# Layer norm's small chain in tensor-and-scalars operations, second half's loads moved up in the first stage, MLP gate's modulation on TensorE

## The chip, the cores and the metric

The kernel runs on one core of one Trainium2 chip. The metric is the device time of one execution in microseconds (us); lower is better. The engines of the core work at the same time, each through its own list of instructions in order, and wait for one another by semaphores: PE (TensorE, matrix products), DVE (VectorE), ACT (ScalarE), POOL (GpSimd) and SP (SyncE, which starts the transfers, DMAs).

## The reference

One step of a trunk of two layers over 128 context tokens and 512 latent tokens with 1024 features. A layer is a mixer and an MLP, each followed by a layer norm, and each modulated by (shift, scale, gate) rows that come from a conditioning vector through a large matrix. Cut to what matters here:

```python
mod_ctx = einsum('d,lde->le', silu(c_ctx), w_mod) + b_mod       # 6*1024 per layer, for the context
mod_lat = einsum('bd,lde->lbe', silu(c), w_mod) + b_mod         # and for the latents
def _layer_norm(x, g, b, eps=1e-5):
    mu, var = mean(x), mean(square(x - mu))
    return (x - mu) * rsqrt(var + eps) * g + b
def _block(x, mod, mixer, g, b, w1, w2):
    sh1, sc1, gt1, sh2, sc2, gt2 = split(mod, 6)                # kinds 0 to 5 below
    x = _layer_norm(ALPHA * x + gt1 * mixer(x * (1 + sc1) + sh1), g[0], b[0])
    ff = square(relu((x * (1 + sc2) + sh2) @ w1)) @ w2
    return _layer_norm(ALPHA * x + gt2 * ff, g[1], b[1])
```

The mixer of layer 0 (the even mixer) is retention beside differential attention, that of layer 1 (the odd mixer) is windowed attention with a sink beside gated linear attention (GLA), whose gates are summed up by scans in chunks of 16 tokens. All of it is in float32.

## The kernel before

The 640 tokens are five tiles of 128, t = 0 the context and t = 1 to 4 the latents. The program runs in stages: a start, the even mixer with its output projection, five layer norms, the MLP in eight groups, five norms, and the same for layer 1 with the odd mixer. The stages overlap at the seams, tile by tile.

Every large product is taken as three products of rounded parts, hi x hi, lo x hi and hi x lo. So each weight unit of 512 KB (`wraw`, three buffers) is split after it has landed: ACT casts the hi part (`whi`), DVE subtracts to get the lo part (`wlo`). Activations are split in the same way (`h0h` and `h0l`, `hh` and `hl`, and in the MLP `ghi` and `glo` from `relu`, the squared ReLU that DVE forms).

**Order of the work.** Nearly all instructions are recorded by helpers, so most rows carry one of few lines: 380 for DVE, ACT and POOL, 470 for matmuls, 485 for transposes, 454 for transfers. The order on PE, DVE, ACT and POOL comes from a planner (class `Order`) that follows a simulated clock while the program is written out. Chains of small steps are generators; a function `background` feeds in weight loads, splits and modulation steps when the clock is due: a modulation step every `MOD_SPACE` = 3.6 us, a chunk on PE every `MOD_PE` = 38 us of that clock. The start stage is different: its instructions stand on ACT, DVE and POOL in the order in which they are written (`order.fifo`). The transfers' queue on SP is ordered by a scheduler.

**Modulation rows.** A row of one kind has two chunks of 512 columns, and a chunk takes eight tiles of weights of 256 KB. Kinds 0 and 1 of layer 0 are made on PE in the start stage (`matvec`, weights `wmod` of the first half and then of the second half, results `mod`). Kinds 2, 3 and 4 of layer 0 are made on PE in the background of the even mixer (`ModPE`: two blocks of 16 small matmuls for a chunk, `modp`, from four buffers `wmodp`). All else (kind 5 of layer 0, the whole of layer 1, 14 chunks) is made by multiplying and adding on POOL, DVE and ACT (`ModChunk`: `wmod` times a column `cs` on POOL, added into `moda` on POOL; for the other accumulator one DVE operation `moda` in layer 1, or ACT `modp` and a POOL addition in layer 0), and summed over partitions by matmuls `modps`. Kind 5 of layer 0 is the gate of the first MLP, needed towards its end.

**Start stage.** The loads, splits and modulated tiles are written out by hand. The first half of the features is modulated (kind 1 and 0) and multiplied early (`early_part`) while the second half's modulation weights arrive.

**Layer norm.** `norm` takes statistics on DVE, the square root on ACT, and then refines 1 / sqrt(var + eps) by one Newton step on columns of [128, 1]: `r`, `q`, `r` again, and `nmr` = -mean * r. The large multiplies that follow (`x` times r plus nmr, then times and plus the rows `lnrow`) are shared by ACT, POOL and DVE. Only at the very end (`final`) are all five tiles written out at once; in the other norms, the next stage starts from the normalised tiles, and `x<-x,lnrow` is done later by POOL to rebuild the residual.

## Time and profile before

| | |
|---|---|
| time, median of 3 runs | 1669.2 us (1667.19 to 1670.53) |
| profiled execution's own time | 1671.51 us |
| its span, first to last instruction | 1669.7 us |
| mean granted clock of PE | 0.979 |
| busy, PE | 1579.6 us, 95% |
| busy, DVE | 1046.0 us, 63% |
| busy, ACT | 619.9 us, 37% |
| busy, POOL | 582.2 us, 35% |

The profiled execution has its own time, 1.8 us longer than its span. Matmuls are pipelined, so PE's busy share is a share of time and not of its peak. The granted clock is that of PE, as a share of full speed. The stages by their place in the span: start 0 to about 65 us, even mixer to about 330, its output projection and norms, first MLP from about 400 to 826, odd mixer from about 880 to 1130, second MLP to about 1651, and the last norms to the end.

### The profile page before, as it was taken

The page shows a single profiled execution, that of the slowest core. Times are in us where ns is not written, and L with a number is a line of the kernel's source. Part 1 is how long each engine was busy: PE and PEld are TensorE (multiplying, and loading weights), DVE is VectorE, ACT ScalarE, POOL GpSimd, SP SyncE. Part 2 cuts the span into 40 slices and gives each one's busy share as a digit, 9 for nine tenths or more (in the row PEclk, how much of TensorE's full clock was granted, in tenths as well). Part 3 has the DMA queues.
Part 4 walks back from the last instruction along what each step waited for, and adds up shares of the span by engine and source line. Part 5 has one row for each costly group of instructions (what it writes and reads, how often), then busy time and mean ns, then how long its engine had stood idle before and what let it go on. Part 6 is the DMA issues. An engine that isn't in the chain of part 4 may idle for free. (4 is left out here: it accounts for less than half of the span.)

```text
span 1669.7 us, 28365 instructions
## 1 busy us (share of the span) xinstructions
PE 1579.6 (95%) x11233; PEld 1431.6 (86%) x11233; DVE 1046.0 (63%) x1963; ACT 619.9 (37%) x1294; POOL 582.2 (35%) x493
## 2 busy tenths in 40 slices
PE   7999999999999999999898898979999999999995
PEld 4998999998989988998787887869989989998994
DVE  3777762685377667767877787777833334444458
ACT  2555443336433312221265454553543222222221
POOL 1110000111896687678557445340200110011215
PEclk9999999999999999999998998989999999999998
DMA  9523333332444444543424210014222221223121
GB/s 345 185 86 93 97 112 105 130 115 64 137 148 151 146 146 152 171 148 106 146 80 137 73 36 28 27 56 141 76 72 68 76 89 60 72 79 115 55 76 63
DMA packets 89764, 177.87 MB, mean 107 GB/s; under 512 B 23576, under 2 KB 30752, under 8 KB 89632
## 3 DMA queue, kind: packets, MB, share of 16 engines
q1 hardware_dynamic: 89632, 176.07, 32.6%
q8 instruction: 88, 1.44, 0.3%
q14 instruction: 44, 0.36, 0.1%
HBM read 169.53 MB, written 6.50 MB: 105 GB/s over the span
## 5 line engine op out<-in xcount | busy, mean ns | idle before, releaser
L470 PE MATMUL ff<-hh,whi 128*128 128x320 f32 (+2 forms) x960 | 297.1, 309 | 0.0
L470 PE MATMUL ff<-hh,wlo 128*128 128x320 f32 (+2 forms) x960 | 296.4, 309 | 0.1
L470 PE MATMUL ff<-hl,whi 128*128 128x320 f32 (+2 forms) x960 | 296.3, 309 | 0.0
L380 DVE TENSOR_TENSOR wlo<-wraw,whi 128x1024 fp32r<-128x1024 f32 (+1 forms) x183 | 243.3, 1334 | 80.4 <-ACT whi L380 80.2
L380 ACT CAST whi<-wraw 128x1024 fp32r<-128x1024 f32 (+1 forms) x183 | 189.5, 1045 | 278.8 <-PE fps L470 244.7
L470 PE MATMUL fps<-whi,glo 128*128 128x512 f32 (+1 forms) x648 | 254.3, 393 | 5.1 <-DVE glo L380 5.1
L470 PE MATMUL fps<-wlo,ghi 128*128 128x512 f32 (+1 forms) x648 | 253.7, 391 | 2.3 <-DVE wlo L380 2.3
L470 PE MATMUL fps<-whi,ghi 128*128 128x512 f32 (+1 forms) x648 | 254.9, 393 | 0.0
L380 POOL TENSOR_TENSOR x<-x,lnrow 128x512 f32<-128x512 f32 (+1 forms) x76 | 105.9, 1402 | 351.6 <-DVE y L380 214.5
L380 DVE TENSOR_TENSOR relu<-relu 128x320 f32<-128x320 f32 (+3 forms) x100 | 70.7, 707 | 186.6 <-ACT ghi L380 185.6
L470 PEld LDWEIGHTS ff<-hh,whi 128*128 128x128 f32 x960 | 180.2, 188 | 3.1 <-issue 2.1
L470 PEld LDWEIGHTS ff<-hl,whi 128*128 128x128 f32 x960 | 180.2, 188 | 0.6
L470 PEld LDWEIGHTS ff<-hh,wlo 128*128 128x128 f32 x960 | 180.2, 188 | 0.3 <-DVE wlo L380 0.3
L380 ACT ACTIVATE relu<-ff 128x320 f32<-128x320 f32 (+3 forms) x100 | 51.4, 514 | 278.7 <-PE ff L470 276.2
L380 DVE TENSOR_TENSOR y<-fps,y 128x512 f32<-128x512 f32 x120 | 82.7, 689 | 111.6 <-PE fps L470 111.5
L470 PEld LDWEIGHTS fps<-whi,glo 128*128 128x128 f32 x648 | 122.1, 188 | 33.2 <-DVE glo L380 5.5
L380 POOL TENSOR_TENSOR moda<-moda,wmod 128x512 f32<-128x512 f32 x98 | 146.0, 1490 | 6.8
L470 PEld LDWEIGHTS fps<-wlo,ghi 128*128 128x128 f32 x648 | 122.1, 188 | 30.3 <-DVE wlo L380 3.5
L470 PEld LDWEIGHTS fps<-whi,ghi 128*128 128x128 f32 x648 | 122.0, 188 | 29.0 <-issue 2.5
L380 POOL TENSOR_SCALAR wmod<-wmod,cs 128x512 f32<-128x512 f32 x98 | 112.7, 1150 | 92.8 <-DVE moda L380 81.4
L380 POOL TENSOR_TENSOR o<-o,sg 128x640 f32<-128x640 f32 x8 | 13.0, 1621 | 257.7 <-ACT o L380 257.3
L470 PE MATMUL proj<-whi,hh 128*128 128x256 f32 (+1 forms) x280 | 85.1, 304 | 12.5 <-DVE gm L380 7.6
(298 smaller groups left out, 3527.7 us busy)
## 6 DMA issues: line engine op xcount, KB each, us to landing
wraw<-in_w SPq DMA_DIRECT2D x128, 512.0 KB
wmod<-in_w_mod SPq DMA_DIRECT2D x144, 256.0 KB
wraw<-in_w_even SPq DMA_DIRECT2D x24, 512.0 KB
wmodp<-in_w_mod SPq DMA_DIRECT2D x48, 256.0 KB
wraw<-in_w_out SPq DMA_DIRECT2D x16, 512.0 KB
wraw<-in_w_odd SPq DMA_DIRECT2D x16, 512.0 KB
gate<-mrow SPq DMA_DIRECT2D x16, 256.0 KB
xT<-in_xT SPq DMA_DIRECT2D x8, 320.0 KB
```

Of the source, the lines that this page charges most:

```text
L380: i = f(*a, **k)
L470: nc.tensor.matmul(o, a, b, **kw)
```

## The change

Three edits. In `norm`, the steps on [128, 1] columns beside the square root are written with one tensor and scalars (constants or columns) each, and one of them is no longer needed: before `ve`, a reciprocal, `q`, `q` again, `r` and `nmr`, of which the last four read two tensors; now `veh`, a reciprocal in place, `q`, `r` and `nmr`. In the start stage, one unit's load and the row `dl` (for lambda, the factor of the differential attention) are asked for after the second half's modulation weights and `xT`, and the splits of the third and fourth unit and `lam` are done later. Kind 5 of layer 0 goes from `ModChunk` to `ModPE`, with `MOD_PE` 30 in place of 38. The diff:

```diff
@@ -37,9 +37,8 @@
 NSPL = 5
 DEC0, DEC = 0.0, 2.0
 MOD_SPACE = 3.6
-MOD_PE = 38.0
+MOD_PE = 30.0
 LO_POOL = 0
-DRS = False
 UPD = 30.0
 WD = 3
 WS = 2
@@ -412,7 +411,6 @@
     const = ctx.enter_context(tc.tile_pool(name="const", bufs=1))
     hpool = ctx.enter_context(tc.tile_pool(name="hpool", bufs=4))
     gpool = ctx.enter_context(tc.tile_pool(name="gpool", bufs=NSLOT))
-    mtmp = ctx.enter_context(tc.tile_pool(name="mtmp", bufs=1))
     mraw = ctx.enter_context(tc.tile_pool(name="mraw", bufs=MRAW))
     wraw = ctx.enter_context(tc.tile_pool(name="wraw", bufs=NRAW))
     wspl = ctx.enter_context(tc.tile_pool(name="wspl", bufs=NSPL))
@@ -596,13 +594,7 @@
                 act.activation(a0, raw, AF.Copy, scale=cs[:, k, 0:1])
                 pool.tensor_scalar(a1, raw, cs[:, k, 1:2], 0.0, op0=ALU.mult, op1=ALU.add)
             else:
-                if self.l == 0:
-                    tmp = mtmp.tile([P, 512], F32, tag="modp", name=nm("modp"))
-                    order.reuse("modp", 1, tmp)
-                    act.activation(tmp, raw, AF.Copy, scale=cs[:, k, 0:1])
-                    pool.tensor_tensor(a0, a0, tmp, op=ALU.add)
-                else:
-                    stt(a0, raw, cs[:, k, 0:1], a0, op0=ALU.mult, op1=ALU.add)
+                stt(a0, raw, cs[:, k, 0:1], a0, op0=ALU.mult, op1=ALU.add)
                 pool.tensor_scalar(raw, raw, cs[:, k, 1:2], 0.0, op0=ALU.mult, op1=ALU.add)
                 pool.tensor_tensor(a1, a1, raw, op=ALU.add)
             if k == KT - 1:
@@ -703,17 +695,15 @@
                 add_piece((l, "2", g, n), [Unit(io["w_2"][l, g, n, u], 2, 512) for u in range(2)])
     pos = [0, 0, 0]
     mod_steps = []
-    for l, kinds in ((0, (5,)), (1, range(6))):
-        if l < layers:
-            for c in kinds:
-                for a in range(2):
-                    chunk = ModChunk(l, 2 * c + a)
-                    mod_steps += [(chunk, k) for k in range(KT)]
+    for c in range(6 if layers > 1 else 0):
+        for a in range(2):
+            chunk = ModChunk(1, 2 * c + a)
+            mod_steps += [(chunk, k) for k in range(KT)]
     mod_left = [0.0, len(mod_steps)]
     mod_hold = [False]
     split_hold = [False]
 
-    mod_pe = [ModPE(2 * c + a) for c in (2, 3, 4) for a in range(2)]
+    mod_pe = [ModPE(2 * c + a) for c in (2, 3, 4, 5) for a in range(2)]
 
     def load_unit():
         units[pos[2]].load()
@@ -944,23 +934,14 @@
         for i, (a, c0, c1) in enumerate(cuts):
             dve.bn_stats(st[:, i, :], X[t][a][:, c0:c1])
         dve.bn_aggr(mv, st)
-        if DRS:
-            ve = sm("ve", [P, 1])
-            dve.tensor_scalar(ve, mv[:, 1:2], EPS, None, op0=ALU.add)
-            r = rsqrt(ve, [P, 1])
-        else:
-            ve = sm("ve", [P, 1])
-            sq = sm("sq", [P, 1])
-            act.activation(sq, mv[:, 1:2], AF.Sqrt, bias=eps_t)
-            dve.tensor_scalar(ve, mv[:, 1:2], EPS, None, op0=ALU.add)
-            r = sm("r", [P, 1])
-            q = sm("q", [P, 1])
-            dve.reciprocal(r, sq)
-            vec_tt(q, r, r, op=ALU.mult)
-            stt(q, q, -0.5, ve, op0=ALU.mult, op1=ALU.mult)
-            stt(r, q, 1.5, r, op0=ALU.add, op1=ALU.mult)
-        nmr = sm("nmr", [P, 1])
-        stt(nmr, mv[:, 0:1], -1.0, r, op0=ALU.mult, op1=ALU.mult)
+
+        veh, sq, q, r, nmr = (sm(n, [P, 1]) for n in ("veh", "sq", "q", "r", "nmr"))
+        act.activation(sq, mv[:, 1:2], AF.Sqrt, bias=eps_t)
+        dve.tensor_scalar(veh, mv[:, 1:2], EPS, -0.5, op0=ALU.add, op1=ALU.mult)
+        dve.reciprocal(sq, sq)
+        dve.tensor_scalar(q, sq, sq, veh, op0=ALU.mult, op1=ALU.mult)
+        dve.tensor_scalar(r, q, 1.5, sq, op0=ALU.add, op1=ALU.mult)
+        dve.tensor_scalar(nmr, mv[:, 0:1], -1.0, r, op0=ALU.mult, op1=ALU.mult)
         if not final:
             xn = X[t]
             for a in range(2):
@@ -1103,19 +1084,19 @@
     load_unit()
     xt = load_x(0)
     load_unit()
-    load_unit()
     ps = acc("mod0")
     for k in range(KT):
         matvec(0, k, ps)
     row = mod_row(ps)
     split_unit()
+    for k in range(KT):
+        load_mod0(1, k)
+    xt1 = load_x(1)
+    load_unit()
     load_unit()
     dls = slot("dl")
     bc_row(dls[:, :256], io["diff_lam"])
     bc_row(sk, io["swa_sink"])
-    for k in range(KT):
-        load_mod0(1, k)
-    xt1 = load_x(1)
     load(cst[:, C_RC:], io["consts"][:, C_RC:])
     mod_cols(0, row)
     order.give()
@@ -1124,9 +1105,6 @@
     split_unit()
     for t in range(1, NT):
         modulated(0, xt, t)
-    split_unit()
-    split_unit()
-    lam(dls)
     ps = acc("mod0")
     for k in range(KT):
         for t in range(NT):
@@ -1141,6 +1119,10 @@
     load_unit()
     for t in TURN:
         modulated(1, xt1, t)
+        if t == TURN[0]:
+            split_unit()
+            split_unit()
+    lam(dls)
     start.close()
     order.give()
     order.fifo = False
```

The planner then makes another order. At three places it is shown as the instructions stand in the program, before and after; a name's number is that of its buffer's use, and L380 of before is L379 of after.

First place: DVE at the end of the first MLP. `wlo` is the split of a weight unit, `relu` and `glo` belong to the last group, `moda` is a step of layer 1's modulation. Before:

```order
L380 TENSOR_TENSOR glo_8755<-relu_1482_8826,ghi_8754 128x640
L380 SCALAR_TENSOR_TENSOR moda_8798<-wmod_8763,cs,moda_8798 128x512
L380 SCALAR_TENSOR_TENSOR moda_8798<-wmod_8796,cs,moda_8798 128x512
L380 TENSOR_TENSOR relu_1489_8893<-relu_1489_8893 128x640
L380 TENSOR_TENSOR glo_8757<-relu_1489_8893,ghi_8756 128x640
L380 SCALAR_TENSOR_TENSOR moda_8798<-wmod_8864,cs,moda_8798 128x512
L380 TENSOR_TENSOR wlo_8934<-wraw_8728,whi_8933 128x1024
L380 TENSOR_TENSOR relu_1492_8928<-relu_1492_8928 128x320
L380 TENSOR_TENSOR glo_8759<-relu_1492_8928,ghi_8758 128x320
L380 SCALAR_TENSOR_TENSOR moda_8798<-wmod_8898,cs,moda_8798 128x512
L380 TENSOR_TENSOR brow_8732<-modps_8972,brow_8732 128x256
```

After:

```order
L379 SCALAR_TENSOR_TENSOR moda_8629<-wmod_8776,cs,moda_8629 128x512
L379 SCALAR_TENSOR_TENSOR x_4589<-x_4589,y_5542 128x512
L379 TENSOR_TENSOR wlo_8874<-wraw_8697,whi_8873 128x1024
L379 TENSOR_TENSOR wlo_8908<-wraw_8774,whi_8907 128x1024
L379 TENSOR_TENSOR relu_1486_8901<-relu_1486_8901 128x640
L379 TENSOR_TENSOR glo_8838<-relu_1486_8901,ghi_8837 128x640
L379 TENSOR_TENSOR relu_1492_8963<-relu_1492_8963 128x640
L379 TENSOR_TENSOR glo_8840<-relu_1492_8963,ghi_8839 128x640
L379 TENSOR_TENSOR wlo_8999<-wraw_8813,whi_8998 128x1024
L379 TENSOR_TENSOR relu_1494_8993<-relu_1494_8993 128x320
L379 TENSOR_TENSOR glo_8842<-relu_1494_8993,ghi_8841 128x320
```

The steps `moda` that stood among the last `relu` and `glo` now stand ahead of them; the first row of the second piece is the last `moda` of the program. The splits `wlo` stand ahead of the `relu` as well.

Second place: POOL in the odd mixer. `x<-x,lnrow` rebuilds the residual, `wmod` and `moda` are modulation steps, `gA` is the buffer of GLA's scans, which DVE runs (they stand in its list as SCALAR_TENSOR_TENSOR `gA<-ones,ge`, and as TENSOR_TENSOR_SCAN in the trace), `Eq` the first use of their result. Before:

```order
L380 TENSOR_SCALAR moda_9907<-wmod_9859,cs 128x512
L380 TENSOR_SCALAR wmod_9867<-wmod_9867,cs 128x512
L380 TENSOR_TENSOR x_4428<-x_4428,lnrow_9062 128x512
L380 TENSOR_TENSOR moda_9907<-moda_9907,wmod_9867 128x512
L380 MEMSET gA_9947 128x5
L380 MEMSET gA_9955 128x5
L380 TENSOR_TENSOR x_4428<-x_4428,lnrow_9066 128x512
L380 TENSOR_TENSOR x_4285<-x_4285,lnrow_9060 128x512
L380 TENSOR_SCALAR wmod_9904<-wmod_9904,cs 128x512
L380 TENSOR_TENSOR x_4285<-x_4285,lnrow_9064 128x512
L380 TENSOR_TENSOR moda_9907<-moda_9907,wmod_9904 128x512
L380 TENSOR_SCALAR wmod_9910<-wmod_9910,cs 128x512
```

After:

```order
L379 TENSOR_TENSOR x_4371<-x_4371,lnrow_9108 128x512
L379 TENSOR_TENSOR x_4371<-x_4371,lnrow_9112 128x512
L379 TENSOR_TENSOR x_4546<-x_4546,lnrow_9110 128x512
L379 MEMSET gA_9966 128x5
L379 MEMSET gA_9974 128x5
L379 TENSOR_TENSOR x_4546<-x_4546,lnrow_9114 128x512
L379 TENSOR_TENSOR x_4401<-x_4401,lnrow_9108 128x512
L379 TENSOR_TENSOR x_4401<-x_4401,lnrow_9112 128x512
L379 TENSOR_TENSOR x_4589<-x_4589,lnrow_9110 128x512
L379 TENSOR_TENSOR x_4589<-x_4589,lnrow_9114 128x512
L379 TENSOR_TENSOR Eq_10137<-gA_9974 128x5x64
```

No modulation step is left between the multiplies of `x`, and `Eq` follows right behind them.

Third place: DVE in the start stage, from the end of the first half's splits. `first_mod` and `sc` are the second half's modulation, `h0h` and `h0l` a modulated tile's parts, `dl` to `nsink` the work of `lam`. Before:

```order
L380 TENSOR_TENSOR wlo_309<-wraw_162,whi_308 128x1024
L380 TENSOR_TENSOR wlo_313<-wraw_203,whi_312 128x1024
L380 TENSOR_TENSOR dl_205<-dl_205 128x128
L380 TENSOR_REDUCE ls<-dl_205 128x2
L380 TENSOR_TENSOR nlam<-ls 128x1
L380 TENSOR_SCALAR nlam<-nlam 128x1
L380 TENSOR_SCALAR nsink<-sink 128x8
L380 TENSOR_TENSOR first_mod<-modT_453,vec 128x2x2x2 x2
L380 TENSOR_SCALAR sc_104<-first_mod 128x8
L380 CAST h0h_106<-h_73_485 128x4x128
L380 TENSOR_TENSOR h0l_108<-h_73_485,h0h_106 128x4x128
```

After:

```order
L379 TENSOR_TENSOR first_mod<-modT_436,vec 128x2x2x2 x2
L379 TENSOR_SCALAR sc_101<-first_mod 128x8
L379 CAST h0h_103<-h_69_468 128x4x128
L379 TENSOR_TENSOR h0l_105<-h_69_468,h0h_103 128x4x128
L379 TENSOR_TENSOR wlo_476<-wraw_238,whi_475 128x1024
L379 TENSOR_TENSOR wlo_480<-wraw_240,whi_479 128x1024
L379 CAST h0h_103<-h_74_483 128x4x128
L379 TENSOR_TENSOR h0l_105<-h_74_483,h0h_103 128x4x128
L379 CAST h0h_103<-h_75_490 128x4x128
```

The two `wlo` were ahead of `first_mod` and now stand behind the first modulated tile of the second half; `dl` to `nsink` come after the fifth such tile.

## Rows read from the trace of the kernel before

**Rows 1.** Totals of PE's waits: what waited for whom, us in total, times, longest.

```profile
PE proj L470 <- DVE gm L380: 7.6, 1, 7.6
PE fps L470 <- DVE glo L380: 5.1, 1, 5.1
...
PE gl L470 <- DVE gST L380: 2.9, 1, 2.9
...
PE fps L470 <- DVE wlo L380: 2.3, 2, 1.3
```

**Rows 2.** Busy time by stretch: length, then each engine, PE's clock, DMA share, GB/s.

```profile
37.00:64.00 27.00, 27.00 (x239) 26.11 (x239) 15.34 (x33) 9.63 (x25) 7.14 (x10) 1.00 0.72 255
400.00:600.00 200.00, 200.00 (x1115) 177.60 (x1114) 122.45 (x129) 69.41 (x101) 145.50 (x113) 1.00 0.43 135
...
813.00:820.00 7.00, 1.93 (x9) 1.27 (x8) 6.93 (x9) 1.95 (x3) 4.55 (x5) 0.76 0.63 175
...
1618.00:1625.00 7.00, 7.00 (x43) 6.43 (x42) 2.05 (x5) 2.76 (x5) 0.00 (x0) 1.00 0.00 0
...
913.00:919.00 6.00, 5.89 (x27) 5.90 (x28) 4.17 (x6) 0.37 (x2) 6.00 (x6) 0.50 0.79 243
...
880.00:1130.00 250.00, 217.18 (x2165) 193.22 (x2165) 191.51 (x400) 120.94 (x308) 124.78 (x138) 0.91 0.19 61
70.00:330.00 260.00, 251.55 (x2310) 241.49 (x2310) 166.53 (x507) 110.63 (x298) 7.93 (x5) 0.99 0.34 104
```

**Rows 3.** DVE's time line in the odd mixer, the scans: start, duration, operation, count.

```profile
900.51 10.31 DVE L380 TENSOR_TENSOR_SCAN gA<-ones,ge 128x128 f32<-128x128 f32 x10
...
930.66 1.68 DVE L380 TENSOR_TENSOR_SCAN gA<-ones,ge 128x128 f32<-128x128 f32 x5
```

**Rows 4.** DVE's time line in the last norms, and POOL's.

```profile
1642.32 1.24 DVE L380 TENSOR_TENSOR q<-r 128x1 f32<-128x1 f32 x1
...
1647.07 0.15 DVE L380 TENSOR_SCALAR ve<-mv 128x1 f32<-128x1 f32 x1
...
1657.16 1.21 DVE L380 TENSOR_TENSOR q<-r 128x1 f32<-128x1 f32 x1
...
1663.69 0.15 DVE L380 TENSOR_TENSOR q<-r 128x1 f32<-128x1 f32 x1
...
1645.07 5.94 POOL L380 TENSOR_TENSOR x<-x,lnrow 128x512 f32<-128x512 f32 x4 [1.53 <-ACT x L380]
```

**Rows 5.** The page: GB/s of the DMA in 40 slices of the span.

```profile
GB/s 345 185 86 93 97 112 105 130 115 64 137 148 151 146 146 152 171 148 106 146 80 137 73 36 28 27 56 141 76 72 68 76 89 60 72 79 115 55 76 63
```

**Rows 6.** PE's time line in the start stage; in brackets idle time before and its releaser.

```profile
27.68 2.59 PE L470 MATMUL mod<-wmod,cs 128*32 128x256 f32 x16 [1.74 <-DMA wmod<-in_w_mod]
...
39.83 1.50 PE L470 MATMUL mod<-wmod,cs 128*32 128x256 f32 x24
```

**Rows 7.** DVE's time line in the start stage.

```profile
34.61 1.23 DVE L380 TENSOR_TENSOR wlo<-wraw,whi 128x1024 fp32r<-128x1024 f32 x1 [3.87 <-ACT whi L380]
35.75 0.28 DVE L380 TENSOR_TENSOR dl<-dl 128x128 f32<-128x128 f32 x1
...
46.63 0.74 DVE L380 TENSOR_TENSOR h0l<-h,h0h 128x512 fp32r<-128x512 f32 x1
```

**Rows 8.** PE's time line in the even mixer, a block of `ModPE`.

```profile
110.94 1.08 PE L470 MATMUL modp<-wmodp,cs 128*32 128x128 f32 x32
```

**Rows 9.** DVE's time line at the end of the first MLP and of the second.

```profile
812.08 1.78 DVE L380 SCALAR_TENSOR_TENSOR moda<-wmod,cs,moda 128x512 f32<-128x512 f32 x1
...
815.64 1.55 DVE L380 TENSOR_TENSOR relu<-relu 128x320 f32<-128x320 f32 x1
...
1619.60 0.49 DVE L380 TENSOR_TENSOR relu<-relu 128x320 f32<-128x320 f32 x1 [2.50 <-ACT ghi L380]
```

**Rows 10.** PE's time line at the end of the first MLP.

```profile
820.76 0.63 PE L470 MATMUL fps<-wlo,ghi 128*128 128x512 f32 x1
...
825.37 0.40 PE L470 MATMUL fps<-whi,ghi 128*128 128x512 f32 x1
```

## Prediction

> **What bounds the kernel now.** I read the page first: PE is busy almost throughout, so time can only come from where it stands still or runs at half clock, or from the ends of the span, where it has no work. So next came the totals of PE's waits [rows 1] and the busy time by stretch [rows 2]. The reader is to see three kinds of stretch there. Between 400 and 600 us, in the first layer's MLP, PE is busy for 200.00 of 200 us: whatever the other engines are spared there is worth nothing. At the seam of that MLP, 813 to 820 us, PE works for 1.93 of 7 us, although the same seam of the second layer, 1618 to 1625 us, is 7.00 of 7. And in the odd mixer, 880 to 1130 us, PE stands still for 250.00 - 217.18 = 32.8 us, with DVE busy for 191.51 us and POOL for 124.78 us. The waits name the same two places: 7.6 us for `gm`, 5.1 us for `glo`, 2.9 us for `gST`, all from DVE. Last came the time lines of DVE, POOL and ACT around each place that the edits touch. Behind the last matmuls DVE works nearly without a gap to the end: the tail is DVE's.
>
> **One behaviour that several terms need.** When POOL multiplies or adds two tensors, a DVE operation with two tensors runs long. Ten scans took 10.31 us, 1.03 us each, under POOL's multiplies, and five took 1.68 us, 0.34 us each, when POOL was idle [rows 3]. The last norm's one-element `q<-r` takes 0.15 us at 1663.69 us, and 1.24 us at 1642.32 us, in one of the stretches of some 6 us in which POOL multiplies four pairs of tensors back to back (the next begins at 1645.07 us) [rows 4]. So a step taken off POOL shortens DVE too.
>
> **The change, part by part.**
>
> *Second half's loads, start stage.* One 512 KB unit and the 128 KB of `dl` leave the queue ahead of the second half's sixteen loads. At the 345 GB/s of the span's first slice of 41.7 us [rows 5] 640 KB are 1.9 us. PE is paced by these loads: sixteen `mod` matmuls took 2.59 us behind a wait of 1.74 us for them, where 24 of them unhindered took 1.50 us [rows 6]; and from 37 us on PE never stands still (27.00 of 27 us [rows 2]), so a gain here carries through: -1.9. Against it, the lo parts of units three and four now stand on DVE behind the first tile's `h0h` and `h0l` instead of being done at 34.61 us, in DVE's idle time. DVE ends that pair at 47.37 us, each lo part takes 1.23 us [rows 7], and PE's first matmuls of the second half need the first of them: about 1.2 us of new wait. The five small operations of `lam` (the first and longest kind 0.28 us [rows 7], so at most 1.4 us) move too, behind the other tiles' `h0l` and ahead of the first ropes. I cost them at nothing, since PE then has the whole first pass of the four products ahead; uncovered they are the 1.4. I take **-0.8**, between -1.9 and +0.7.
>
> *Kind 5 of layer 0 on PE, even mixer.* Two more chunks make four more blocks of 16 matmuls (32 in the trace, which counts each twice). A block takes 1.08 us [rows 8], of which I count 1.0, since the next matmul starts before its modelled end. PE is busy for 251.55 of 260 us there [rows 2], so all of it lies on the path: 4 x 1.0 = **+4.0**. The lower bound is 0, if the blocks fall into the 8.4 us of waits; the upper is +11, if each of the four waits as long for its weights as PE did for `wmod` at the start, 1.74 us [rows 6]. The before trace has no wait of PE for a `wmodp` load, so I take the middle value. The DVE additions of four bias rows lie beside PE's work.
>
> *The same kind off POOL, ACT and DVE, first MLP.* 98 - 84 = 14 pairs of POOL steps, and the fourteen ACT and POOL steps of layer 0, go; PE is full there: **0**.
>
> *What that does at the seam.* The list of POOL and DVE steps is a seventh shorter and ends before the seam instead of in the odd mixer; in the order of after no `moda` stands behind the last two `wlo` of the MLP. Before, DVE's last groups ran among them: a `moda` of 1.78 us, a `relu` of 1.55 us, against 0.49 us in the second layer [rows 9]. PE waited 5.1 us for `glo` and 1.3 us for `wlo` [rows 1], and after the stall it ran at a lower clock (granted 0.76 over 813 to 820 [rows 2]; a matmul of 0.63 us at 820.76 us against 0.40 at 825.37 us [rows 10]): eight such matmuls lost up to 8 x 0.23 = 1.8 us. 5.1 + 1.3 + 1.8 = 8.2. I take **-6.5**, since the durations of successive matmuls overlap and a short wait for a last `wlo` may stay, between 0 (the stall has another cause) and -8.2.
>
> *What that does in the odd mixer.* POOL no longer mixes `wmod` and `moda` with its `x` multiplies, which then run at once and end before the scans, and DVE loses its `moda` steps there. If the ten scans take 0.34 instead of 1.03 us, DVE comes 6.9 us earlier to `gm`, for which PE waited 7.6 us [rows 1]. After that wait PE had 6 us at a granted clock of 0.50 [rows 2], which is the lower of its two levels (1.2 of 2.4 GHz): 5.89 us of matmuls that take half at the full level, 2.9. Adding the wait of 2.9 us for `gST`, which stands behind the same DVE work, 7.6 + 2.9 + 2.9 = 13.4. DVE remains busy for three quarters of this stretch and feeds PE at other places too, so some of it will turn up as a wait further on. I take **-10**, three quarters, between -2 (the waits stay, and only steps that DVE and POOL run outside them go) and -13.4.
>
> *Norm chain, between the stages.* One operation fewer in each chain, of the 0.15 us that `q<-r` takes undisturbed [rows 4]. Three of the four sets of norms lie before a stage that starts with them; two of the five tiles each may stand on the path, so 3 x 2 x 0.15 = **-0.9**; the bounds are 0 and 3 x 5 x 0.15 = -2.3.
>
> *Norm chain, tail.* Four of the one-element operations of two tensors were stretched from 0.15 to between 1.21 and 1.25 us, first and last at 1642.32 and 1657.16 us [rows 4]: 4 x 1.07 = 4.3 us. The new ones have one tensor and scalars that are [128, 1] columns. An operation of one tensor and constants at 1647.07 us, within POOL's multiplies of 1645.07 to 1651.01 us, took 0.15 us [rows 4]. Whether a column for a scalar counts as a second tensor no row shows. If it does, only the operation removed is gained, 5 x 0.16 = -0.8; if not, 4.3 + 0.8 = -5.1. But a wait that goes here partly moves to the next addition of two tensors, `x<-x,tmp`, which meets the same multiply: I take half, **-2.6**.
>
> The sum is -0.8 + 4.0 + 0 - 6.5 - 10 - 0.9 - 2.6 = -16.8 us. From the profiled execution's own 1671.5 us (span 1669.7) that gives 1654.7; it was 2.3 us above the median of the runs, 1669.2, so on the median I predict 1669.2 - 16.8, rounded **1652 us**.
>
> **A rule against the tail's term.** The Trainium skill, page "SBUF — State Buffer", section "Who interferes with whom", says that `tensor_scalar` on DVE is among the operations that can enter a mode in which they hold the port pair shared with GpSimd for the whole instruction, so that the new chain would meet POOL just as the old one did. By it the tail would give -0.8 and the sum -15.0, 1654 us. The row at 1647.07 us speaks against it for the one-element form.
>
> **Rivals.**
> - *The odd mixer gives it back.* DVE is busy for 191.5 of 250 us, and more than half of PE's 32.8 us of idle time there belongs to other waits than the two for `gm` and `gST` (7.6 + 2.9), which no part of the change touches. If only 2 of the 10 us stay, the sum is -8.8: about 1660 us. For it: DVE's share. Against it: the wait of 7.6 us and the half clock behind it are one event with one cause.
> - *The new scalars wait like tensors* (the mechanism of the bound above): tail -0.8, sum -15.0, about 1654 us.
> - *The stalls are not the modulation's.* At the seam and at `gm` other work (the weights' lo parts, POOL's `x` multiplies) is also among the long operations. If both stalls stay, the sum is -0.8 + 4.0 - 0.9 - 2.6 = -0.3, and with the odd mixer's least gain of 2: about 1667 us, no change.
> - *Slower: the even mixer's PE queue waits for weights.* Eight chunks of two blocks, started 30 instead of 38 us apart on the planner's clock, share four buffers of `wmodp`; PE's queue is in order, so a block whose weights are late holds all that is behind it. To eat up 16.8 us and lose 3.5 more, 20 us, each of the sixteen has to wait 1.3 us: about 1673 us. For it: the other twelve blocks move to other places as well, and the whole stage's order of steps with them. Against it: the trace has no such wait for twelve blocks, and the stretch has DMA to spare (share 0.34 of 70 to 330 us [rows 2]).
>
> **How the numbers follow.** A measurement of this kernel tells 0.2% (3.3 us) from no change. Forecast 0.60, given back 0.20, scalars 0.05, stalls not the modulation's 0.07, slower 0.08. Faster by over 0.2% are the first three, 0.85; same 0.07; slower 0.08. The forecast's own range is 1646 to 1659: down by the odd mixer's -13.4 and the tail's -5.1 together, up by the even mixer's +11. The second case at 1660, with some of the even mixer's bound on top, moves the upper end to 1664, the seam's -8.2 the lower one to 1644; the last two cases stay outside.
>
> **What would show it.** Right: PE busy for over 6 of 7 us at the seam near 810 us and no wait for `glo` over 2 us; scans near 0.35 us and no wait for `gm` over 3 us; no `wmod` on POOL after the seam; in the tail one-element operations of the norm at 0.15 us throughout; PE's first even-mixer matmul of the second half about 1 us earlier. Wrong: a wait of PE for `wmodp`, more than 9 us added between 70 and 330 us, a wait for `gm` that only changes its name, or the tail's `x<-x,tmp` longer by what the chain lost.

## The result, and the profile after

The changed kernel runs at a ratio of 0.9857 to the kernel before (95% interval 0.9836 to 0.9878), 23.9 us of 1668.9. The predicted 1652 us would be a ratio of 0.990; the measured time, 0.9857 x 1669.2 = 1645 us, lies near the lower end of the stated 1644 to 1664 and just below the forecast's own range, which began at 1646. Three runs, of 1642.56 to 1646.97 us, are behind this ratio; a fourth took 1671.83 us at a granted clock of 0.911 and is left out. The profiled execution took 1642.56 us (span 1640.8), the fastest of the runs, and the one of before, at 1671.51 us, lies above all its runs, so their differences add up to -28.9 us and not to -23.9.

To see where they lie I divide every trace by the first and last products of each stage on PE's time line. The second row is the measure for what follows; stages in us. One trace each is compared: the eight traces with the start stage of before have their first even-mixer product at 60.3 to 62.4 us, so differences of 1 to 2 us in a stage are not told from scatter.

| kernel | start, to first even-mixer product | even mixer, to the MLP | first MLP | odd mixer, to the MLP | second MLP | tail | span |
|---|---|---|---|---|---|---|---|
| before | 61.5 | 314.9 | 474.0 | 346.1 | 455.0 | 18.3 | 1669.7 |
| after | 65.5 | 316.6 | 467.4 | 320.7 | 455.8 | 14.8 | 1640.8 |
| difference | +4.0 | +1.7 | -6.6 | -25.4 | +0.8 | -3.5 | -28.9 |
| predicted | -0.8 | +4.0 | -6.5 | -10 | -0.9 in all norms | -2.6 | -16.8 |

PE's waits after, which answer to [rows 1]: totals, times, longest.

```profile
PE sd L468 <- DVE qkh L379: 5.9, 3, 3.1
PE proj L468 <- DVE sg L379: 5.7, 1, 5.7
PE early L468 <- ACT v L379: 3.6, 1, 3.6
...
PE fps L468 <- DVE wlo L379: 2.0, 2, 1.0
```

The waits for `gm`, `glo` and `gST`, 15.6 us together before, have no row any more. New are a wait of 5.7 us late in the odd mixer and one of 3.6 us in the start stage, for ACT's copy of `v`.

Busy time by stretch after, which answers to [rows 2] (the first row is the odd mixer from its first product, 0.6 us later than in the table; the third is the start):

```profile
850.20:1170.23 320.03, 299.52 (x2887) 273.89 (x2885) 245.73 (x561) 167.41 (x425) 132.60 (x142) 0.97 0.23 75
...
813.00:820.00 7.00, 7.00 (x45) 6.64 (x44) 4.18 (x11) 2.67 (x6) 0.00 (x0) 1.00 0.85 254
...
44.00:66.00 22.00, 17.37 (x131) 16.96 (x130) 16.50 (x32) 9.25 (x23) 7.84 (x8) 0.92 0.50 158
70.00:330.00 260.00, 250.22 (x2404) 237.90 (x2403) 165.66 (x507) 113.96 (x306) 8.06 (x5) 1.00 0.37 118
```

The same view of before for the odd mixer as a whole:

```profile
851.00:1196.42 345.42, 307.91 (x2903) 281.31 (x2901) 264.17 (x578) 168.01 (x427) 154.95 (x161) 0.94 0.23 76
```

The reader is to see three things. The seam is filled: PE is busy for 7.00 of 7 us where it was 1.93. The odd mixer lost 25.4 us in two ways: PE stands still for 20.5 instead of 37.5 us (-17.0), and its busy time fell from 307.9 to 299.5 us (-8.4) for nearly the same instructions, at a granted clock of 0.97 instead of 0.94. At most 1.3 us of that are sixteen `modps` matmuls, which the changed kernel does in the first MLP. And the start, where PE never stood still before, has PE busy for only 17.37 of 22 us.

DVE's time line after, at the seam and at the first scans, which answer to [rows 9] and [rows 3]:

```profile
813.91 0.48 DVE L379 TENSOR_TENSOR relu<-relu 128x320 f32<-128x320 f32 x1
814.43 0.49 DVE L379 TENSOR_TENSOR glo<-relu,ghi 128x320 fp32r<-128x320 f32 x1
...
897.82 1.69 DVE L379 TENSOR_TENSOR_SCAN gA<-ones,ge 128x128 f32<-128x128 f32 x5
```

`relu` takes 0.48 instead of 1.55 us and a scan 0.34 instead of 1.03 us.

DVE's time line in the tail after, and POOL's, which answer to [rows 4]:

```profile
1615.57 1.53 DVE L379 TENSOR_TENSOR x<-x,tmp 128x512 f32<-128x512 f32 x1
1617.02 0.26 DVE L379 TENSOR_SCALAR q<-sq,veh 128x1 f32<-128x1 f32 x1
...
1622.21 0.26 DVE L379 TENSOR_SCALAR q<-sq,veh 128x1 f32<-128x1 f32 x1
...
1618.71 15.28 POOL L379 TENSOR_TENSOR x<-x,lnrow 128x512 f32<-128x512 f32 x10 [0.46 <-ACT x L379]
```

No one-element operation of the norm is over 0.27 us, in the middle of POOL's multiplies. `x<-x,tmp` is still stretched: 1.53 us here, 1.48 us at the same place before, so the wait that left the chain did not move there.

### The profile page after: what moved, and what is told of

The parts are those of the page before. It is cut to its first block, busy times and chain, and to the rows that moved or that the text cites. A ratio compares the mean times of both kernels' runs of the same rounds, so it can differ in the third digit from the quotient of the medians.

```text
span 1640.8 us, 28521 instructions
## 1 busy us (share of the span) xinstructions
PE 1573.2 (96%) x11345; PEld 1425.5 (87%) x11345; DVE 1020.2 (62%) x1945; ACT 610.0 (37%) x1278; POOL 525.8 (32%) x449
## 4 chain that ended last, share of the span: by engine, by line
PE 85%; DVE 7%; ACT 4%; DMA 1%; POOL 1%; issue 1%; SPq 0%; POOLq 0%; DVEq 0%; ACTq 0%
PE ff L468 26%; PE fps L468 26%; PE proj L468 12%; PE ops L468 6%; PE fproj L468 3%; ACT h L379 1%; PE sd L468 1%; PE early L468 1%; PE odp L468 1%; PE po L468 1%; DMA wmod<-in_w_mod 1%; PE modp L468 1%; PE gl L468 1%; DVE x L379 1%; PE ss L468 1%
## 5 line engine op out<-in xcount | busy, mean ns | idle before, releaser
L379 ACT CAST whi<-wraw 128x1024 fp32r<-128x1024 f32 (+1 forms) x183 | 189.7, 1046 | 279.0 <-PE fps L468 250.2
L379 DVE TENSOR_TENSOR wlo<-wraw,whi 128x1024 fp32r<-128x1024 f32 (+1 forms) x183 | 243.8, 1337 | 73.3 <-ACT whi L379 73.0
L379 POOL TENSOR_TENSOR x<-x,lnrow 128x512 f32<-128x512 f32 (+1 forms) x76 | 107.9, 1432 | 349.1 <-DVE y L379 215.3
L379 DVE TENSOR_TENSOR relu<-relu 128x320 f32<-128x320 f32 (+3 forms) x100 | 64.1, 641 | 189.4 <-ACT ghi L379 185.7
L379 ACT ACTIVATE relu<-ff 128x320 f32<-128x320 f32 (+3 forms) x100 | 51.5, 515 | 295.1 <-PE ff L468 295.1
L379 DVE TENSOR_TENSOR y<-fps,y 128x512 f32<-128x512 f32 x120 | 82.7, 689 | 117.8 <-PE fps L468 117.7
L379 POOL TENSOR_SCALAR wmod<-wmod,cs 128x512 f32<-128x512 f32 x84 | 95.9, 1142 | 123.7 <-DVE moda L379 108.1
L379 POOL TENSOR_TENSOR moda<-moda,wmod 128x512 f32<-128x512 f32 x84 | 124.2, 1478 | 6.3
L468 PE MATMUL proj<-whi,h0h 128*128 128x256 f32 x320 | 92.0, 288 | 0.9 <-DVE catl L379 0.5
```

The source lines that it names most:

```text
L379: i = f(*a, **k)
L468: nc.tensor.matmul(o, a, b, **kw)
```

## The experiments

All ratios are to the kernel before, measured beside it on the same chip. Two theories stood at first: A, that the modulation steps themselves stretch the seam and the odd mixer; B, that each edit makes the planner order the odd mixer anew, and that this is the gain.

**1. The norm alone** (the kernel before with the new lines of `norm`).

> The kernel before with the new norm chain alone. Theory A (the modulation steps are what stretches the seam and the odd mixer; the norm is worth only its own steps): the tail shortens by about 3.5 us, as between the two traces (18.3 to 14.8 us behind the last product), the other norms by up to 1, the seam and the odd mixer stay: ratio about 0.997 (-4 to -5 us). Theory B (each edit makes the planner order the odd mixer anew, and that is the gain): the odd mixer changes by more than 5 us here too.

Measured 0.9992 (0.9978 to 1.0006): the expected 0.997 lies outside the interval. The tail is 15.0 us instead of 18.3, as expected, and the odd mixer is unchanged (346.6 us). In the time 1.3 us of gain are seen, less than the tail's 3.3, which lie inside the interval (-3.7 to +1.0 us). Against B.

**2. The start alone** (the kernel before with the new order of loads, splits and `lam`).

> The kernel before with the new start stage alone. Theory A: second half's products end 1.6 us earlier, but PE then waits 1.0 us for a split and 3.7 us for ACT's copy of v, so the start costs about +3 us and the rest stays: ratio about 1.002. Theory B: as for the norm alone, a change of more than 5 us in the odd mixer.

Measured 1.0045 (1.0031 to 1.0059), more than expected: the start is 67.9 instead of 61.5 us and the even mixer 1.3 us longer. Odd mixer 342.5 us, 3.6 less, under the bound that B asked for. So this edit costs 7.5 us by itself.

**3. Kind 5 on PE alone.**

```diff
-MOD_PE = 38.0
+MOD_PE = 30.0
-    for l, kinds in ((0, (5,)), (1, range(6))):
+    for l, kinds in ((1, range(6)),):
-    mod_pe = [ModPE(2 * c + a) for c in (2, 3, 4) for a in range(2)]
+    mod_pe = [ModPE(2 * c + a) for c in (2, 3, 4, 5) for a in range(2)]
```

> The kernel before with kind 5 of layer 0 on PE alone. Theory A: the even mixer +4 to +5, the seam -7, the odd mixer -20 to -25: about -23 us, ratio 0.986. Theory B: less than half of that, since the other two edits would carry a part of the gain in the odd mixer.

Measured 0.9806 (0.9778 to 0.9833), 32 us, more than all three edits together. First MLP 467.0 us (-7.0), odd mixer 318.2 (-27.9), even mixer 316.9 (+2.0 with its four blocks more). The other two edits had no part in the gain of the odd mixer. Whether this one gains by its own steps or by the new order, experiment 5 tells.

**4. The modulation only denser.**

```diff
-MOD_SPACE = 3.6
+MOD_SPACE = 3.0
```

> The kernel before with MOD_SPACE 3.0 in place of 3.6 and nothing else: kind 5 stays with POOL, DVE and ACT, but all steps end before the seam, without the four blocks on PE. Theory A: seam -7 and odd mixer -20 to -25 as in the changed kernel, even mixer 0: about -28 us, ratio 0.983, unless the denser steps stretch DVE so far in the first MLP that PE waits there. If what counts is the work taken off POOL as such and not where it ends: no more than -7.

Measured 0.9853 (0.9835 to 0.9871). The odd mixer falls to 317.4 us although nothing was taken off POOL: what counts is that no step is left for that stage. But the first MLP grows to 477.9 us, although its seam has no wait for `glo` any more. DVE's and PE's time lines of this kernel show one of the places:

```profile
528.09 1.18 DVE L380 SCALAR_TENSOR_TENSOR moda<-wmod,cs,moda 128x512 f32<-128x512 f32 x1
532.17 0.75 DVE L380 SCALAR_TENSOR_TENSOR moda<-wmod,cs,moda 128x512 f32<-128x512 f32 x1 [2.91 <-DMA wmod<-in_w_mod]
532.84 0.48 DVE L380 TENSOR_TENSOR relu<-relu 128x320 f32<-128x320 f32 x1
...
534.27 0.80 PE L470 MATMUL fps<-whi,glo 128*128 128x512 f32 x1 [4.42 <-DVE glo L380]
```

A `moda` at the head of DVE's list waits 2.91 us for its weights, `relu` and `glo` are queued behind it, and PE waits 4.42 us.

**5. The steps of the odd mixer planned, but not written.** This separates the steps' own work from the order that the planner makes. The program leaves out nine of the ten steps, a DVE and two POOL instructions each (the traces have 75 `moda` on DVE instead of 84); the tenth, the first of its chunk, runs on ACT and POOL and stays. PE, ACT and all else keep the order of before:

```diff
+            if self.order.skip:
+                x.ins = None
+                return None
             i = f(*a, **k)
...
                 else:
+                    order.skip = odd[0]
                     stt(a0, raw, cs[:, k, 0:1], a0, op0=ALU.mult, op1=ALU.add)
                 pool.tensor_scalar(raw, raw, cs[:, k, 1:2], 0.0, op0=ALU.mult, op1=ALU.add)
                 pool.tensor_tensor(a1, a1, raw, op=ALU.add)
+                order.skip = False
...
             mod_hold[0] = False
+            odd[0] = True
```

> The kernel before, planned as before, but the ten modulation steps (one DVE and two POOL operations each) that it places in the odd mixer aren't written into the program; everything else stands in the same order. The sums of two modulation rows of layer 1 are left incomplete by that. Theory A1 (the steps' own time on DVE and POOL and the stretching they cause make PE wait): the odd mixer, 345.4 us from its first product to the first of the next MLP, shortens by 10 or more, and PE's wait for gm falls under 2 us. Theory A2 (the other order of steps, which the planner makes when no modulation is left for this stage, is the gain): under 5 us shorter, and the waits after 1000 us stay as they are. The seam near 815 us stays in both.

Measured 0.9890 (0.9859 to 0.9920). The odd mixer, counted from its first product:

```profile
849.32:1174.49 325.17, 301.40 (x2902) 275.23 (x2901) 245.84 (x570) 167.92 (x427) 134.58 (x143) 0.97 0.23 75
```

```profile
896.36 3.26 DVE L385 TENSOR_TENSOR_SCAN gA<-ones,ge 128x128 f32<-128x128 f32 x10
```

325.2 instead of 345.4 us: 20.2 of the 25.4 us are the nine steps and what they stretch, A1. The ten scans, in the same order, take 3.26 us instead of 10.31. DVE is busy for 18.3 us less (264.17 to 245.84): half of that are the nine `moda`, 9.2 us together in the trace of before, and half the shorter scans, 7.05 us in these ten. How much of PE's 20.2 us is the steps' own time and how much the stretching, this run does not separate. The wait for `gm` is gone, and so is the one for `gST`. The longest waits after 1000 us stay as they were (3.24 us for `ropea`, 3.46 for `pT`, 3.31 for `sg`), as A2 said. The other 5 us (25.4 - 20.2) are put down to the changed kernel's order, from one trace each. They lie in that later part (185.2 against 180.0 us); from 140 us behind the mixer's first product to its end, before, in experiment 5 and after:

```profile
991.00:1196.42 205.42, 183.97 (x1817) 166.90 (x1815) 158.67 (x387) 95.03 (x244) 71.95 (x78) 0.93 0.19 64
...
989.32:1174.49 185.17, 166.17 (x1648) 152.03 (x1644) 142.61 (x355) 86.01 (x219) 65.79 (x70) 0.94 0.21 68
...
990.20:1170.23 180.03, 165.29 (x1636) 150.54 (x1635) 140.01 (x351) 85.48 (x220) 62.29 (x69) 0.95 0.21 68
```

PE stands still there for 21.5, 19.0 and 14.7 us. The seam's wait of 4.51 us for `glo` is still in experiment 5.

**6. POOL's additions alone, in the changed kernel.**

```diff
+        if fill and op.ins.name == fill[0]:
+            i = nc.gpsimd.memset(fl, 0.0)
+            for _ in range(9):
+                tc.add_manual_dep(i.ins, last.ins.name, mybir.DependencyInfo(
+                    mybir.DependencyClass.NoSync, mybir.DependencyReason.DATA), reason="order")
+                last = i
+                if _ < 8:
+                    i = nc.gpsimd.tensor_tensor(fl, fl, fl, op=ALU.add)
```

> The changed kernel with eight additions of 128x512 that compute nothing needed, put on POOL ahead of the first Eq of the odd mixer, where POOL waits for the scans for 10.6 us; no other instruction moves. Eight take 10.3 us undisturbed. If POOL's two-tensor work stretches DVE's scans (theory A1): scans of about 1.0 instead of 0.34 us, ge and the splits longer, DVE's chain some 5 us later, and PE again waits for gm or Eq: +4 to +9 us, half clock behind it included. If only order and DVE's own work count: within 1 us, since POOL was idle there.

Measured 0.9845 (0.9816 to 0.9874), the changed kernel's own ratio. A miss, and a telling one. DVE's time line and POOL's:

```profile
901.79 5.62 DVE L379 TENSOR_TENSOR_SCAN gA<-ones,ge 128x128 f32<-128x128 f32 x5
...
909.18 1.68 DVE L379 TENSOR_TENSOR_SCAN gA<-ones,ge 128x128 f32<-128x128 f32 x5
911.26 1.63 DVE L379 TENSOR_SCALAR gm<-z,vec 128x320 f32<-128x320 f32 x3 [0.40 <-ACT ge L379]
...
896.90 10.23 POOL L466 TENSOR_TENSOR fl<-fl 128x512 f32<-128x512 f32 x8
```

In the changed kernel the same step is:

```profile
907.29 1.63 DVE L379 TENSOR_SCALAR gm<-z,vec 128x320 f32<-128x320 f32 x3 [4.34 <-ACT ge L379]
```

The stretching was there: five of the mixer's twenty scans took 1.12 us under POOL's additions, 0.34 us behind them. It cost 3.9 us of DVE's time, which DVE had: its idle time before `gm` fell from 4.34 to 0.40 us, and PE saw nothing. So stretching of this size, at this place, has no price by itself. Before, it came on top of DVE's own modulation steps in the same stretch; that the two together used up DVE's idle time fits experiments 5 and 6, but no run adds stretching without steps over the whole stretch.

**7. Where the start's loss comes from.** The changed kernel with `lam` and its row as before; the unit's load and the splits stay moved.

```diff
+    dls = slot("dl")
+    bc_row(dls[:, :256], io["diff_lam"])
+    bc_row(sk, io["swa_sink"])
     for k in range(KT):
         load_mod0(1, k)
...
         modulated(0, xt, t)
+    lam(dls)
     ps = acc("mod0")
```

> The changed kernel with lam and the load of its row back ahead of the second half; the unit's load and the splits stay moved. If PE's wait of 3.65 us for v comes from ACT, whose copies stand behind the exponential of lam and wait for DVE with it: that wait and the half clock behind it go, -4 to -6 us against the changed kernel, less 0.4 for the row's 128 KB. If it comes from the splits of units three and four: no change (within 1 us).

Measured 0.9843 (0.9812 to 0.9875), not told apart from the changed kernel. The time lines of ACT and PE in the changed kernel:

```profile
53.58 0.20 ACT L379 ACTIVATE ls<-ls 128x2 f32<-128x2 f32 x1 [5.28 <-DVE ls L379]
53.69 0.35 ACT L379 COPY qk<-early 128x256 f32<-128x256 f32 x1
53.95 1.05 ACT L379 CAST whi<-wraw 128x1024 fp32r<-128x1024 f32 x1
54.89 0.43 ACT L379 COPY v<-early 128x128 f32<-128x128 f32 x2
...
37.17 1.50 PE L468 MATMUL mod<-wmod,cs 128*32 128x256 f32 x24
...
45.89 0.39 PE L468 MATMUL early<-wlo,h0h 128*128 128x256 f32 x1 [0.98 <-DVE wlo L379]
55.38 0.58 PE L468 MATMUL early<-whi,h0h 128*128 128x256 f32 x1 [3.65 <-ACT v L379]
```

and PE's in experiment 7:

```profile
39.69 1.50 PE L468 MATMUL mod<-wmod,cs 128*32 128x256 f32 x24
...
57.96 0.39 PE L468 MATMUL early<-whi,h0h 128*128 128x256 f32 x1 [0.86 <-ACT v L379]
```

The exponential of `lam` stands on ACT ahead of the copies that free PE's results, and it waits 5.28 us for DVE, where `lam` stands behind five tiles. Without it the wait is 0.86 instead of 3.65 us, so ACT's queue is the cause of most of it. The second half's products, with the row ahead of their loads, end at 41.2 instead of 38.7 us in these two traces (38.7 to 40.0 in the four traces with the whole of the new loads' order). The start becomes 63.8 instead of 65.5 us, still 2.2 longer than before. That the time didn't fall with it is the even mixer's doing, which takes 319.9 instead of 316.6 us here; experiment 8 shows its rows.

**8. The old start stage with the other two edits.** (The three hunks of the start stage in the diff are undone.)

> The changed kernel with the whole start stage of before: kind 5 on PE and the new norm chain alone. From the single parts (ratio 0.9806 for kind 5, tail -3.4 us in the trace of the norm alone): about -35 us, ratio 0.979, faster than the changed kernel by the 4 to 7 us that its start stage costs.

Measured 0.9788 (0.9758 to 0.9817), as expected, and 0.9775 (0.9751 to 0.9799) on the chip of experiment 11:

> The kernel with kind 5 on PE, the new norm and the start stage of before once more, on the same chip as the one with the late row: ratio 0.979 again, and the measure for that one.

This kernel beats both. Its start is 62.4 and 60.3 us in the two traces, its even mixer 314.1 us in both, its odd mixer 319.6 and 318.7.

It was measured beside experiment 7, which differs from it only in the place of the unit's load and of the two splits: 1635.0 against 1643.1 us by the medians. In the traces most of that lies behind the start stage, although the edit ends there. The even mixer as a whole: before, experiment 3, this kernel, the changed kernel, experiment 7:

```profile
61.53:376.38 314.85, 303.74 (x2768) 292.07 (x2767) 209.14 (x601) 135.24 (x354) 17.41 (x13) 0.99 0.35 109
...
60.89:377.81 316.92, 308.55 (x2896) 296.14 (x2895) 208.75 (x605) 135.60 (x355) 17.25 (x13) 0.99 0.38 122
...
62.40:376.47 314.07, 305.71 (x2896) 293.16 (x2895) 208.36 (x602) 135.69 (x355) 17.17 (x13) 1.00 0.39 124
...
65.55:382.13 316.58, 305.70 (x2897) 292.84 (x2895) 209.74 (x602) 135.90 (x355) 17.16 (x13) 1.00 0.38 122
...
63.76:383.71 319.95, 306.18 (x2897) 292.88 (x2895) 210.09 (x602) 135.66 (x355) 17.01 (x13) 1.00 0.39 122
```

At the same granted clock PE stands still for 8.4 us with the old start, 10.9 us in the changed kernel and 13.8 us in experiment 7.

**9. `lam` left to the planner, its row late.**

```diff
-    lam(dls)
     start.close()
     order.give()
     order.fifo = False
+    order.begin()
+    lam(dls)
```

> The changed kernel with lam left to the planner behind the start stage, so that its exponential no longer stands on ACT ahead of the copies of v, while the row's load stays late. If lam on ACT is what costs in the new start stage: PE's wait of 3.65 us for v and the half clock behind it go, the first product of the even mixer comes at 60 to 62 us instead of 65.6, and the time falls 4 to 6 us under the changed kernel's (ratio 0.982 to 0.983), unless the planner's new order of the even mixer takes some of it. If the splits of units three and four cost it: within 1 us of the changed kernel at that place.

Measured 0.9847 (0.9832 to 0.9862), no gain over the changed kernel. The wait for `v` fell to 1.43 us and the start to 62.3 us (-3.2), but the even mixer took 322.8 us. Some of that isn't the planner's: experiment 6 has the very order of the changed kernel up to the odd mixer, and its even mixer took 320.3 instead of 316.6 us. The even mixer of experiment 9 and of experiment 6:

```profile
62.30:385.14 322.84, 308.90 (x2896) 295.49 (x2895) 208.45 (x602) 136.15 (x355) 17.14 (x13) 0.99 0.38 121
...
65.89:386.20 320.31, 309.44 (x2896) 296.35 (x2895) 209.88 (x602) 135.75 (x354) 17.14 (x13) 0.98 0.37 120
```

Experiment 6 stands still no longer than the changed kernel (10.9 us) but is busy for 3.7 us more, at a lower granted clock. Of the 8.8 us by which experiment 9 is longer than experiment 8, 5.6 are standing still (13.9 against 8.4 us) and 3.2 are busy time at a lower granted clock. The changed kernel and experiment 6 around one of the waits:

```profile
156.00:176.00 20.00, 16.88 (x168) 15.71 (x167) 13.86 (x30) 12.09 (x30) 0.00 (x0) 1.00 0.18 54
```

```profile
156.00:176.00 20.00, 16.80 (x148) 15.28 (x148) 13.00 (x28) 10.76 (x26) 0.00 (x0) 0.83 0.17 53
```

Both have a wait of PE of 3.1 us there (for `qkh`, a wait that is 1.21 us with the old start). In one execution the granted clock stayed at the upper of its levels behind it, in the other it did not. That makes one even mixer from a single trace uncertain by some 4 us.

**10. The tail: two tensors or one operation fewer.** The best kernel of experiment 8 with

```diff
-        dve.tensor_scalar(q, sq, sq, veh, op0=ALU.mult, op1=ALU.mult)
-        dve.tensor_scalar(r, q, 1.5, sq, op0=ALU.add, op1=ALU.mult)
-        dve.tensor_scalar(nmr, mv[:, 0:1], -1.0, r, op0=ALU.mult, op1=ALU.mult)
+        stt(q, sq, sq, veh, op0=ALU.mult, op1=ALU.mult)
+        stt(r, q, 1.5, sq, op0=ALU.add, op1=ALU.mult)
+        stt(nmr, mv[:, 0:1], -1.0, r, op0=ALU.mult, op1=ALU.mult)
```

> Kind 5 on PE and the new norm with five operations, with the start stage of before, but with q, r and nmr written as operations of two tensors (the same count and order). If the tail's gain comes from no longer waiting for POOL with two tensors: the tail behind the last product, 14.8 us with the new chain and 18.3 with the old, goes back to 17 to 18 us, and one-element operations of over 1 us are seen again. If it comes from the one operation fewer: it stays at 15. In the time that is +0.15% at most over the same kernel with one tensor and scalars (ratio 0.9788).

Measured 0.9811 (0.9797 to 0.9824). That is 0.2 to 0.4% above the same kernel with one tensor, where 0.15% at most was expected; the intervals overlap and the chips differ, so the excess is not shown. The tail is 17.7 us, against 14.8 there:

```profile
1616.26 1.24 DVE L379 SCALAR_TENSOR_TENSOR q<-sq,veh 128x1 f32<-128x1 f32 x1
1617.53 1.21 DVE L379 SCALAR_TENSOR_TENSOR r<-q,sq 128x1 f32<-128x1 f32 x1
```

So some 2.8 of the 3.5 us are the second tensor, and the other 0.7 go with the operation that is gone.

**11. The row of lambda late, all else of the old start.** (Experiment 8 with the lines of `dls` behind `load_x(1)` and `lam` as in experiment 9.)

> Kind 5 on PE, the new norm and the start stage of before, with one thing of the new start: the row of lambda is loaded behind the second half's loads, and lam is left to the planner behind the start stage; the unit's load and the splits of units three and four stay where they were. If the row, which is written to all 128 partitions, is what delays the second half: its products end at about 39 instead of 40 to 42 us, the first product of the even mixer comes 1 to 2 us earlier than with the old start, and the time is 1 to 2 us under that kernel's, if the even mixer keeps its order (it nearly does). If the unit's 512 KB are what delays it: no change.

Measured 0.9800 (0.9776 to 0.9824), on the chip on which the old start gave 0.9775: slower, not faster, by the medians 1637.1 against 1633.2 us. The second half's products end at 39.6 us in this trace, 0.5 before those of the old start on the same chip. But the old start's eight traces have them at 40.1 to 42.1 us, so whether the row or the unit delays them is not told. PE waits for `v` again:

```profile
55.74 0.38 PE L468 MATMUL early<-whi,h0h 128*128 128x256 f32 x1 [1.51 <-ACT v L379]
```

## Why the prediction was right, and where it was not

The time fell inside the range and on the side that was forecast. Not all of that is merit: two terms lie outside their own bounds, one on each side. By its terms:

- **The end of the first MLP: -6.5 predicted, -6.6 measured.** Mechanism and size as forecast: `relu` back at 0.48 us, no wait for `glo`, and only 1.02 us of the wait for `wlo` left.
- **The odd mixer: -10 predicted, -25.4 measured, outside its bounds of -2 and -13.4; the term was mis-sized.** The mechanism is shown by experiment 5, where the order stays: 20.2 us come from nine steps and the stretching. Two things were missing in the working. The bound of -13.4 took the half clock of one stretch, 2.9 us; in experiment 5, with the matmuls of before, PE's busy time in the mixer fell by 6.5 us (307.91 to 301.40) as the granted clock rose from 0.94 to 0.97. And the reduction to three quarters, for waits that turn up again further on, was the wrong way round: in the later part PE stands still for 14.7 instead of 21.5 us. So the change did touch the other waits, which the rival of the gain given back took as untouched; that rival did not happen.
- **The even mixer: +4.0 predicted, +1.7 in the trace, +2.0 with that edit alone.** Experiment 3 shows the parts at the granted clock of before (0.99): PE is busy for 4.8 us more (303.74 to 308.55), so the blocks did lie on the path as priced, and stands still for 2.7 us less (11.1 to 8.4), which the term had not. The 314.1 us with the old start and the new norm, under the 314.9 of before, are no sign that the blocks fell into waits: PE stands still as long as in experiment 3, and its busy time is 2.8 us shorter at a granted clock of 1.00. No wait for `wmodp` was seen, so the rival on the slow side didn't occur.
- **The start: -0.8 predicted, +4.0 measured. This step was wrong.** The wait for the split was right (0.98 us, predicted 1.2), and the loads' gain was of the size forecast: the second half's products end at 38.7 instead of 41.3 us in this pair of traces (2.7, predicted 1.9), and at 38.7 to 40.0 against 40.1 to 42.1 over all traces of either start. What failed is "I cost them at nothing", said of `lam`: I looked at DVE, on which its operations are short, and not at ACT, on which the exponential waits with the copies of `v` behind it. PE waited 3.65 us, and from 54 to 60 us at a granted clock of 0.72. `lam` and its row moved alone cost 3.8 us (experiment 11 against the old start on the same chip). But `lam` is the smaller part: with it back in place (experiment 7) the kernel is still 8.1 us behind the old start by the medians. There the unit's load and the two splits are moved, the start is 1.4 us longer in the traces, and the even mixer 5.9 us, of which PE stands still for 5.4. The term had nothing for what the start stage's order does to the stage behind it. What the whole edit costs was measured as 0.45 to 0.8% of the time: 1.0045 for it alone, and 0.9857 with it against 0.9788 and 0.9775 without.
- **The tail: -2.6 predicted, -3.5 measured.** Right in mechanism, by experiment 10; the reason for taking half, a wait that moves to `x<-x,tmp`, did not show (1.48 us before, 1.53 after). The rule in the Trainium skill's page "SBUF — State Buffer", section "Who interferes with whom", by which `tensor_scalar` could have held the port pair shared with GpSimd, did not show: with a column as scalar the one-element form took 0.20 to 0.27 us under POOL's multiplies, somewhat longer than the 0.15 us of the old forms undisturbed, and never over a microsecond. Its sentence on instructions with two SBUF inputs, which contend with GpSimd's reads, is what experiments 6 and 10 show (1.12 against 0.34 us, 1.24 against 0.26 us).
- **The other norms: -0.9 predicted.** Nothing that a trace tells from its scatter; the second MLP and its norms came out 0.8 us longer.

The errors of the start (4.8 us too good) and of the odd mixer (15.4 us too bad) have opposite signs, which is why the sum, -16.8 against -28.9 in the traces and -23.9 in the runs, came nearer than the odd mixer's term. That is luck.

What stays open: which of the moved pieces, the unit's load or the splits, makes PE's waits in the even mixer longer (10.9 to 13.9 us against 8.4), and why the granted clock behind the same wait differed between executions, which adds up to 3.7 us.

## What to carry to other kernels

Background work that is cheap on average is dear where it is left over for a stage that feeds PE through one busy engine: look at where its list ends, not at its sum. When an instruction is moved on a queue written by hand, follow each of its parts on every engine; the shortest one, an exponential of 0.20 us, made the longest new wait of its stage, since it waited at the head of another engine's queue. Then look at the stage behind: an order written by hand moves its waits too. A stretched operation costs only what exceeds its engine's idle time before the next consumer, as in experiment 6.

## What the runs showed of the hardware

- A DVE operation of two tensors runs long under POOL's two-tensor work even with one element per partition (1.24 us for `q<-sq,veh`), while the form with one tensor and column scalars does not (0.26 us).
- The granted clock over the 20 us around a wait of PE of 3.1 us was 1.00 in the changed kernel and in experiment 7, 0.91 in experiment 9 and 0.83 in experiment 6, which has the changed kernel's order there. The even mixers of the changed kernel and of experiment 6 differ by 3.7 us with it.
